# One group's input ahead of the heads, the other two beside the first projections

## The chip, the cores and the metric

One core of a Trainium2 chip runs the kernel. The core has five engines, each with its own queue of instructions: TensorE (PE: matrix multiplications and transposes, from SBUF into PSUM), VectorE (DVE), ScalarE (ACT), GpSimd (POOL) and SyncE (SP), which here only issues DMA transfers between HBM and SBUF. The metric is the device time of one execution in microseconds.

## What is computed

One streaming step of a small encoder of two layers, on 2048 rows of a prompt and 8 x 16 rows of samples, each row 1024 wide (17 tiles of 128 rows: 16 of the prompt, one of the samples). The part that matters here is the first layer, a gated DeltaNet with 8 heads:

```python
ada = c_act @ p["w_ada"][i] + p["b_ada"][i]
shift, scale, gate = jnp.split(ada[:, None, :], 3, axis=-1)
h = (rmsnorm(x, p["norm_pre"][i]) * (1.0 + scale) + shift)
# gdn_mixer
proj = h @ w_in                       # q, k, v (1024 columns each), z (1024), a and b (8 each)
qkv_c, new_buf = causal_conv(qkv, conv_buf, conv_w)
g = -jnp.exp(a_log) * jax.nn.softplus(a + dt_bias)
beta = jax.nn.sigmoid(b)
o, s_new = gdn_chunked(q, k, v, g, beta, s0, ...)   # per head: an inverse per block, then a scan over the blocks
o = rmsnorm(o, o_norm) * jax.nn.silu(z)
y = o @ w_out
```

The second layer is a differential attention; nothing of it is touched.

## The kernel before

The 17 tiles are handled in two halves. The first has nine, in three groups of three: group 0 is prompt tiles 0 and 1 and the sample tile, groups 1 and 2 are prompt tiles 2 to 4 and 5 to 7 (`HALVES`, lines 337 to 345). A half goes through `gdn_heads`, `out_proj`, `diff_heads` and `out_proj` again, each a stage of its own.

**The planner.** All stages are written as generators (streams), run by the class `Weave` (lines 88 to 327). It keeps a modelled time for each engine and each result, takes at every step the stream that can go on earliest (between equals the one with the higher priority, the last argument of `W.spawn`), and writes its instructions down. On PE, DVE, ACT and POOL the instructions run in the order in which they were written; on SP this holds only until `first_start` has ended (`W.ordered = False`, line 770). Places for tiles are rings: a stream that wants one waits until an earlier user has let go (`W.tile`, `W.keep`, `W.free`). `copy` and `either` (lines 206 to 219) choose the engine of a copy or of a subtraction by which is free in the model. `modulate` does so for ACT and DVE.

**The preparation, `first_start` (line 747).** It loads the weights of the adaptation for shift and scale of the first layer, 8 MB as eight transfers of 1 MB into a ring of four (`ada_load`), applies them (`ada_apply`, `ada_end`), and beside that runs `start` (line 729): for all three groups of the half, each tile's x (512 KB) is loaded into a ring of seven (`xn`), scaled by its norm (`scale_rows`: two squares on ACT, three small operations on POOL, one product on DVE), and, when a group's three tiles are there, turned into h: `h_parts` starts eight parts of 128 rows of hT. A part (`h_part`, line 673) transposes on PE into one of two PSUM banks (`TURN`), multiplies and adds (`modulate`, into one of two `htmp`), rounds to a first half (`W.copy`) and subtracts for a second half. The eighth part frees the x (lines 683 to 685). The result of a group is `hT` with the event `("w", "h", 0, half, gi)`. `first_start` also loads the first four of the heads' weight matrices (`gdn_loads(0)[:4]`, eight transfers of 256 KB through the two `st` buffers, each split by DVE, ACT and POOL). The stage ends when all this is written down; `vectors` (line 514) follows, a few small operations.

**The heads, `gdn_heads` (line 955).** `projections` (line 1023) goes over heads, in each over the three groups, in each over k, q, v: for each it waits for the group's hT and for the weights and does 24 matmuls (`mm3s`) into one of two banks (`PROJ`); `conv` then copies the result out into one of three `ub` buffers (`NU`), and convolves on DVE; for the sample tile it waits for the cached rows (`cached`, event `"cc"`). `gate_columns` (line 1060) does the columns of a and b for each of the three groups in turn, and after the third `gate_values` computes all gates (event `"gates"`), on which `keys`, `inverse` and `scans` of every head wait. q and k have five buffers each, freed by the scans. `others` (line 1007, the lowest priority) does the columns of z, 24 matmuls per tile and block, and the adaptation of later use; the weights for these come one after the other into the single place `wz` (`other_loads`, line 999).

Of the kernel before, what the change touches and what calls it, by code (L numbers as in the profile page):

```python
# [12 lines left out]
F32 = mybir.dt.float32  # L13
# [317 lines left out]
def body(ctx, tc, I, O):  # L331
# [341 lines left out]
    def h_part(l, half, gi, kt, xs, hT, temp, left):  # L673
        tiles = HALVES[half][gi]
        nt = len(tiles)
        n = nt * P
        for f in (1, 0):
            yield ("w", "A", l, f, kt // 4),
        ps = yield from bank_of(TURN)
        for i in range(nt):  # L680
            pe.transpose(ps[:, i * P:(i + 1) * P], cols_of(xs[tiles[i]], kt * P, P), ident)
        left["x"] -= 1
        if left["x"] == 0:
            for t in tiles:
                W.free(*(xs[t] if isinstance(xs[t], list) else [xs[t]]))
        ht = yield from temp()
        yield from modulate(l, kt, tiles, ht, ps)
        W.free(ps)
        yield from W.copy(hT[:, 0, kt, 0:n], ht[:, 0:n], n)
        e = W.either(n)  # L690
        yield e
        getattr(W, e).tensor_tensor(out=hT[:, 1, kt, 0:n], in0=ht[:, 0:n], in1=hT[:, 0, kt, 0:n].bitcast(F32),
                                    op=ALU.subtract)
        W.free(ht)
        left["h"] -= 1
        if left["h"] == 0:
            W.done(("w", "h", l, half, gi))
# [31 lines left out]
    def start(half, pool, nx):  # L729
# [10 lines left out]
        for gi, tiles in enumerate(HALVES[half]):  # L740
# [6 lines left out]
    def first_start(pool):  # L747
# [4 lines left out]
        def ada():  # L752
            for i, x in enumerate(todo):
                yield from ada_load(x, *x[2:], pool)
                if i == 0:
                    W.spawn(start(0, pool, 7), 3)
# [79 lines left out]
    def out_proj(l, hi_, groups, pool, ahead):  # L836
# [97 lines left out]
        if more:  # L934
            W.spawn(start(hi_ + 1, pool, 3), 1)
# [19 lines left out]
    def gdn_heads(hi_, tiles_of, pool, ahead):  # L955
# [15 lines left out]
        h_in = [hTs[0, hi_, gi] for gi in range(NGr)]  # L971
# [3 lines left out]
        def used_h(gi):  # L975
            uses[gi] -= 1
            if uses[gi] == 0:
                W.free(h_in[gi])
# [20 lines left out]
        def other_loads():  # L999
            for x in extras[:-1]:  # L1000
# [4 lines left out]
            yield from load_all(ahead[:1])  # L1005

        def others():
            for x in extras:
# [4 lines left out]
                for gi, tiles in enumerate(tiles_of):  # L1013
                    for i, t in enumerate(tiles):
                        ps = yield from bank()
                        yield from mm3s(ps[:, 0:WN], tok(h_in[gi], i), slots[x].cols(0, WN))
# [6 lines left out]
        def projections():  # L1023
            for h in range(H):
                for gi, tiles in enumerate(tiles_of):
# [3 lines left out]
                    for typ in (1, 0, 2):  # L1029
# [4 lines left out]
                                        lambda kt: (h_in[gi][:, 0, kt, 0:n], h_in[gi][:, 1, kt, 0:n]))  # L1034
# [25 lines left out]
        def gate_columns():  # L1060

            ab = pool.tile([P, MAXT, 2 * H], F32, name="ab", bufs=1)
            for gi, tiles in enumerate(tiles_of):
# [4 lines left out]
                for k4 in range(0, KT, 4):  # L1068
                    for i in range(2):
                        for q in range(4):  # L1070
                            pe.matmul(ps[32 * q:32 * q + 32, 0:n], wab[:, k4 + q, :],
                                      h_in[gi][:, i, k4 + q, 0:n].bitcast(F32),
# [556 lines left out]
        W.spawn(other_loads(), 5.5)  # L1629
        W.spawn(scans(), 5)  # L1630
# [562 lines left out]
```

## Time and profile before

| | us |
|---|---|
| median of three runs | 3585.93 |
| lowest, highest | 3585.64, 3587.45 |
| the profiled execution, its own time | 3588.79 |
| its span in the trace | 3587.0 |

Times in the trace are counted from the start of the span. Nearly every instruction is recorded through one helper (line 105), so the rows are told apart by tile names: `xn` is x, `htmp` a part of h before it is split, `hT` the result, `adaw` the adaptation's weights, `st` the staging of other weights, `wab` the weights of the gate columns, `wq` the weights of q, k and v, `wz` those of z. `ps<-hT,wq` is a projection, `ps<-cst_ident,xn` a transpose of x. PE is a matmul, PEld the load of its stationary operand, SPq the issue of a transfer.

### The profile page before, as it was taken

Reading aid. Unit: us, or ns where it says so; the run is one execution under the profiler, and the core shown is the slowest. Engines: PE = TensorE matmul, PEld = TensorE weight load, DVE = VectorE, ACT = ScalarE, POOL = GpSimd, SP = SyncE. Lnnn points to the kernel's source line nnn. Section 1 sums busy time; section 2 is a strip of 40 time slices with the busy share of each in tenths; the row PEclk is TensorE's granted clock in tenths of the full one; section 3 lists DMA queues with packets and bytes.
Section 4 is the critical chain, followed back from the end, with each engine's and each line's share of the span. In section 5 each row is a group of like instructions: output and inputs, shape, how many; then the busy total and the mean of one; then the engine's idle time right before and its main releaser. Section 6 shows DMA issues by size and latency. Waiting matters only on the chain.

```text
span 3587.0 us, 79525 instructions
## 1 busy us (share of the span) xinstructions
PE 3420.1 (95%) x29336; PEld 3178.8 (89%) x29336; DVE 2556.4 (71%) x6345; ACT 1773.7 (49%) x5379; POOL 1622.3 (45%) x2758
## 2 busy tenths in 40 slices
PE   5999999999999999999999999998899999999988
PEld 2887789889999999998989899888899999999988
DVE  4677788775576666666467877775588888888872
ACT  3454455553354444444445555553365555555541
POOL 4344444443444434443344654444455455554442
PEclk6999999999999999999999999999999999999999
DMA  5225422235343333344531222225311112111113
GB/s 190 59 72 158 122 76 73 58 99 189 127 125 108 112 112 115 111 119 120 180 93 47 59 58 75 61 72 162 124 42 55 29 56 57 50 52 34 51 59 124
DMA packets 479420, 330.61 MB, mean 92 GB/s; under 512 B 65799, under 2 KB 442143, under 8 KB 479030
## 3 DMA queue, kind: packets, MB, share of 16 engines
q1 hardware_dynamic: 474358, 316.76, 30.0%
q0 software_dynamic: 4672, 8.78, 1.0%
q8 instruction: 230, 3.77, 0.4%
q14 instruction: 160, 1.31, 0.1%
HBM read 233.65 MB, written 91.77 MB: 91 GB/s over the span
## 4 chain that ended last, share of the span: by engine, by line
PE 75%; DVE 11%; DMA 4%; POOL 4%; ACT 3%; issue 3%; SPq 0%; POOLq 0%; DVEq 0%; ACTq 0%
PE ps L105 75%; DVE negm L105 1%; DVE Lt L105 1%; DVE p L105 1%; POOL p L105 1%; POOL fo L105 1%; DVE wq L105 1%; POOL sm L105 1%; DVE Lr L105 1%; ACT L105 1%; ACT jkg L105 1%; SPq L105 0%; DVE Lw L105 0%; DVE at L105 0%; DVE r L105 0%
## 5 line engine op out<-in xcount | busy, mean ns | idle before, releaser
L105 PE MATMUL ps<-wq,hT 128*128 128x256 f32 x6120 | 853.3, 287 | 4.4 <-DVE r L105 3.4
L105 PEld LDWEIGHTS ps<-wq,hT 128*128 128x128 f32 x6120 | 775.3, 190 | 17.5 <-DVE r L105 4.5
L105 PE MATMUL ps<-hT,wq 128*128 128x384 f32 (+1 forms) x3456 | 697.5, 341 | 2.1 <-ACT ub L105 1.6
L105 PE MATMUL ps<-wz,hT 128*128 128x256 f32 x4488 | 648.8, 291 | 14.2 <-DVE r L105 13.4
L105 PEld LDWEIGHTS ps<-wz,hT 128*128 128x128 f32 x4488 | 581.3, 193 | 23.8 <-DVE r L105 14.8
L105 PEld LDWEIGHTS ps<-hT,wq 128*128 128x128 f32 x3456 | 558.1, 190 | 15.3 <-issue 2.9
L105 ACT ACTIVATE p<-ps,negm 128x512 f32<-128x512 f32 (+3 forms) x640 | 396.9, 624 | 240.5 <-DVE negm L105 235.5
L105 DVE TENSOR_REDUCE negm<-ps 128x1 f32<-128x512 f32 (+3 forms) x640 | 377.7, 606 | 48.3 <-PE ps L105 37.9
L105 POOL TENSOR_SCALAR p<-p,fj 128x512 f32<-128x512 f32 (+2 forms) x320 | 247.1, 782 | 231.8 <-DVE fj L105 179.2
L105 PE MATMUL ps<-kst,qst 128*128 128x512 f32 (+3 forms) x1280 | 347.1, 380 | 0.4 <-ACT p L105 0.4
L105 PE MATMUL ps<-vpc,at 128*128 128x128 f32 x2176 | 294.4, 277 | 4.6 <-DVE at L105 4.0
L105 DVE SCALAR_TENSOR_TENSOR p<-p,fj,p 128x512 f32<-128x512 f32 (+2 forms) x320 | 274.2, 882 | 27.9 <-POOL p L105 27.0
L105 PEld LDWEIGHTS ps<-vpc,at 128*128 128x128 f32 x2176 | 271.4, 192 | 15.2 <-DVE at L105 8.8
L105 PEld LDWEIGHTS ps<-kst,qst 128*128 128x128 f32 x1280 | 206.6, 190 | 18.2 <-ACT p L105 2.7
L105 PE MATMUL ps<-cst_ident,p 128*128 128x128 f32 x1224 | 194.0, 275 | 16.1 <-DVE p L105 12.1
L105 POOL TENSOR_TENSOR wq<-st,wq 128x512 fp32r<-128x512 f32 x103 | 142.6, 1386 | 144.6 <-ACT wq L105 72.4
L105 ACT COPY at<-ps 128x512 f32<-128x512 f32 (+1 forms) x208 | 106.4, 512 | 188.5 <-PE ps L105 187.2
L105 ACT ACTIVATE jk<-ps 128x128 f32<-128x128 f32 (+1 forms) x212 | 80.3, 379 | 229.6 <-PE ps L105 177.2
L105 POOL TENSOR_TENSOR fo<-fo,cpow 128x1 f32<-128x1 f32 x280 | 173.9, 621 | 23.3
L105 PEld LDWEIGHTS ps<-cst_ident,p 128*128 128x128 f32 x1224 | 144.0, 141 | 25.3 <-DVE p L105 15.1
L105 POOL TENSOR_TENSOR r<-r,r 128x256 f32<-128x256 f32 (+1 forms) x144 | 106.2, 758 | 108.5 <-DVE r L105 106.7
L105 POOL TENSOR_SCALAR fo<-so,sm 128x1 f32<-128x1 f32 x136 | 51.0, 375 | 211.2 <-ACT jkg L105 210.9
(334 smaller groups left out, 6519.2 us busy)
## 6 DMA issues: line engine op xcount, KB each, us to landing
st<-in_w_in_gdn_dram SPq DMA_DIRECT2D x128, 256.0 KB
st<-in_w_in_diff_dram SPq DMA_DIRECT2D x256, 128.0 KB
x<-x SPq DMA_DIRECT2D x34, 512.0 KB
wz<-in_w_ada_dram SPq DMA_DIRECT2D x16, 1024.0 KB
sp<-in_cache_k_dram SPq DMA_DIRECT2D x64, 256.0 KB
sp<-in_cache_v_dram SPq DMA_DIRECT2D x64, 256.0 KB
zg<-zt SPq DMA_DIRECT2D x68, 128.0 KB
og<-o SPq DMA_DIRECT2D x136, 64.0 KB
```

What stands on the lines that cost most here:

```text
L105: r = f(*args, **kw)
```

## The change

`first_start` prepares group 0 only, with three x buffers instead of seven. Groups 1 and 2 are prepared in `gdn_heads` by a new stream, `later_start` (priority 6.5), for the first half only. It takes one place that holds all three tiles of a group: for group 1 the place that hT of group 2 is written to later, for group 2 the place `wz`; it issues the three transfers and starts `later_rows` for each tile, which does the same `scale_rows` and `h_parts` as before, with a PSUM bank for the squares and `ub` buffers for the parts in place of `jk` and `htmp`. The eighth part frees the place as a whole (`"held"`). `other_loads` waits for the event that the transfers of group 2 have been issued, and then for `wz` to be free. hT is looked up when it is used, and not when the stage begins. The start of the second half's groups is as before.

```diff
--- before.py
+++ after.py
@@ -681,8 +681,11 @@
             pe.transpose(ps[:, i * P:(i + 1) * P], cols_of(xs[tiles[i]], kt * P, P), ident)
         left["x"] -= 1
         if left["x"] == 0:
-            for t in tiles:
-                W.free(*(xs[t] if isinstance(xs[t], list) else [xs[t]]))
+            if "held" in xs:
+                W.free(xs["held"])
+            else:
+                for t in tiles:
+                    W.free(*(xs[t] if isinstance(xs[t], list) else [xs[t]]))
         ht = yield from temp()
         yield from modulate(l, kt, tiles, ht, ps)
         W.free(ps)
@@ -726,7 +729,7 @@
         return (lambda: W.tile(pool, [P, 512], F32, "jk", 1, "s"),
                 lambda: W.tile(pool, [P, 384], F32, "htmp", 2, "v"))
 
-    def start(half, pool, nx):
+    def start(half, pool, nx, groups):
 
         xs = {}
         junk, temp = norm_places(pool)
@@ -737,7 +740,8 @@
             if not left:
                 yield from h_parts(0, half, gi, xs, temp)
 
-        for gi, tiles in enumerate(HALVES[half]):
+        for gi in groups:
+            tiles = HALVES[half][gi]
             left = set(tiles)
             for t in tiles:
                 x = xs[t] = yield from W.tile(pool, [P, D], F32, "xn", nx, "sy")
@@ -753,7 +757,7 @@
             for i, x in enumerate(todo):
                 yield from ada_load(x, *x[2:], pool)
                 if i == 0:
-                    W.spawn(start(0, pool, 7), 3)
+                    W.spawn(start(0, pool, 3, [0]), 3)
 
         def apply():
             for x in todo:
@@ -932,7 +936,7 @@
         W.spawn(collect(l, hi_, range(len(groups) - 1, len(groups)), 512, [lambda: new([P, 512], "ro", NR, "sy")] * 2,
                         lambda: bank_of(TURN)), 1)
         if more:
-            W.spawn(start(hi_ + 1, pool, 3), 1)
+            W.spawn(start(hi_ + 1, pool, 3, range(len(HALVES[hi_ + 1]))), 1)
         W.spawn(projections(), 0)
         W.run()
 
@@ -968,14 +972,13 @@
         if hi_ == 0:
             v.memset(tailsP, 0.0)
         U, gates = {}, {}
-        h_in = [hTs[0, hi_, gi] for gi in range(NGr)]
         uses = [2] * NGr
         rows_left = {t: H + 4 for ts in tiles_of for t in ts}
 
         def used_h(gi):
             uses[gi] -= 1
             if uses[gi] == 0:
-                W.free(h_in[gi])
+                W.free(hTs[0, hi_, gi])
 
         def row_done(t):
             rows_left[t] -= 1
@@ -997,12 +1000,34 @@
             yield from load(x, w_gdn, [(3072 + x[3] * WN, WN)], kind)
 
         def other_loads():
+            if hi_ == 0:
+                yield ("placed", NGr - 1), "sy"
             for x in extras[:-1]:
                 if x[1] == "ada":
                     yield from ada_load(x, *x[2:])
                 else:
                     yield from z_load(x, "wide")
             yield from load_all(ahead[:1])
+
+        def later_start():
+
+
+            places = (lambda: W.keep("hT2_0", lambda: tails[0].tile([P, 2 * KT * 384], F32, name="hT2", bufs=1), "sy"),
+                      lambda: W.tile(wpool, [P, 2 * KT * WN], F32, "wz", 1, "sy"))
+            for gi, place in zip((1, 2), places):
+                xs = dict(held=(yield from place()))
+                left = set(tiles_of[gi])
+                for i, t in enumerate(tiles_of[gi]):
+                    xs[t] = xs["held"][:, i * D:(i + 1) * D]
+                    sy.dma_start(xs[t], x_rows[t])
+                    W.spawn(later_rows(gi, t, xs, left), 3)
+                W.done(("placed", gi))
+
+        def later_rows(gi, t, xs, left):
+            yield from scale_rows(xs[t], bank)
+            left.remove(t)
+            if not left:
+                yield from h_parts(0, hi_, gi, xs, lambda: new([P, 388], "ub", NU, "v"))
 
         def others():
             for x in extras:
@@ -1013,7 +1038,7 @@
                 for gi, tiles in enumerate(tiles_of):
                     for i, t in enumerate(tiles):
                         ps = yield from bank()
-                        yield from mm3s(ps[:, 0:WN], tok(h_in[gi], i), slots[x].cols(0, WN))
+                        yield from mm3s(ps[:, 0:WN], tok(hTs[0, hi_, gi], i), slots[x].cols(0, WN))
                         W.spawn(gate_out(t, x[3], ps))
                         yield 0
                     if x == extras[-1]:
@@ -1031,7 +1056,7 @@
                         yield (key,)
                         ps = yield from bank_of(PROJ)
                         yield from mm3s(ps[:, 0:n], slots[key].cols(0, P),
-                                        lambda kt: (h_in[gi][:, 0, kt, 0:n], h_in[gi][:, 1, kt, 0:n]))
+                                        lambda kt: (hTs[0, hi_, gi][:, 0, kt, 0:n], hTs[0, hi_, gi][:, 1, kt, 0:n]))
                         if gi == NGr - 1:
                             W.free(slots[key])
                         W.spawn(conv(h, gi, typ, ps, d), 1)
@@ -1069,7 +1094,7 @@
                     for i in range(2):
                         for q in range(4):
                             pe.matmul(ps[32 * q:32 * q + 32, 0:n], wab[:, k4 + q, :],
-                                      h_in[gi][:, i, k4 + q, 0:n].bitcast(F32),
+                                      hTs[0, hi_, gi][:, i, k4 + q, 0:n].bitcast(F32),
                                       start=k4 == 0 and i == 0, stop=k4 > 0 and i == 1)
                 raw = yield from new([P, 384], "nv", NN, "s")
                 s.copy(raw[:, 0:n], ps[:, 0:n])
@@ -1627,6 +1652,8 @@
             W.spawn(cached(), 4)
         W.spawn(loads(), 6)
         W.spawn(other_loads(), 5.5)
+        if hi_ == 0:
+            W.spawn(later_start(), 6.5)
         W.spawn(scans(), 5)
         W.spawn(projections(), 0)
         W.spawn(others(), -1)
```

## Rows read from the trace of the kernel before

**Rows 1.** The page: TensorE over the span, and its granted clock in 40 slices.

```profile
PE 3420.1 (95%) x29336; PEld 3178.8 (89%) x29336; DVE 2556.4 (71%) x6345; ACT 1773.7 (49%) x5379; POOL 1622.3 (45%) x2758
...
PEclk6999999999999999999999999999999999999999
```

**Rows 2.** Stretches: length, busy us of each engine, granted clock, DMA share, GB/s.

```profile
30.00:35.00 5.00, 3.21 (x14) 1.33 (x15) 1.34 (x3) 1.37 (x3) 0.77 (x3) 0.50 1.04 396
...
55.00:69.00 14.00, 7.43 (x26) 4.02 (x24) 11.95 (x21) 6.43 (x13) 9.04 (x10) 0.50 0.26 69
...
60.00:80.00 20.00, 12.82 (x53) 6.94 (x57) 14.19 (x26) 8.86 (x17) 11.00 (x12) 0.50 0.23 64
...
69.00:81.00 12.00, 8.40 (x39) 4.21 (x43) 7.56 (x13) 5.44 (x9) 5.56 (x6) 0.50 0.22 63
...
155.00:265.00 110.00, 108.10 (x1088) 98.42 (x1086) 85.23 (x241) 59.40 (x193) 48.42 (x106) 1.00 0.22 55
```

**Rows 3.** Timeline of SP, 20 to 72 us: start, us, transfers issued, count.

```profile
20.40 5.01 SPq L105 DMA_DIRECT2D xn<-in_x_prompt_dram  x1
...
25.51 0.56 SPq L105 DMA_DIRECT2D adaw<-in_w_ada_dram  x1
...
26.12 3.02 SPq L105 DMA_DIRECT2D xn<-in_x_prompt_dram  x1
...
53.16 17.87 SPq L105 DMA_DIRECT2D st<-in_w_in_gdn_dram  x6
```

**Rows 4.** Timeline of all engines, 37 to 81 us (idle time before in brackets).

```profile
37.77 3.30 PE L105 MATMUL ps<-adaw,cT 128*32 128x512 f32 x16
...
44.39 0.56 ACT L105 ACTIVATE htmp<-ps,adaB,adaA 128x256 f32<-128x256 f32 x1 [1.28 <-DVE adaB L105]
...
56.08 1.50 DVE L105 TENSOR_TENSOR hT<-htmp,hT 128x384 fp32r<-128x384 f32 x1
...
68.22 1.11 POOL L105 TENSOR_TENSOR hT<-htmp,hT 128x384 fp32r<-128x384 f32 x1
...
79.84 0.56 DVE L105 TENSOR_TENSOR hT<-htmp,hT 128x384 fp32r<-128x384 f32 x1 [0.58 <-ACT hT L105]
```

**Rows 5.** Timeline of PE, 77 to 112 us: gate columns and first projections.

```profile
77.97 4.54 PE L105 MATMUL ps<-hT,wab 128*32 128x384 f32 x32
...
85.52 4.71 PE L105 MATMUL ps<-hT,wq 128*128 128x384 f32 x18
...
97.68 2.79 PE L105 MATMUL ps<-hT,wab 128*32 128x384 f32 x32
...
101.76 10.13 PE L105 MATMUL ps<-hT,wq 128*128 128x384 f32 x57
```

**Rows 6.** Timeline of DVE, 102 to 121 us: convolutions of group 0 and, last, group 1.

```profile
102.07 1.52 DVE L105 SCALAR_TENSOR_TENSOR k<-ub,taps,k 128x256 f32<-128x256 f32 x3
...
103.82 1.12 DVE L105 SCALAR_TENSOR_TENSOR k<-us,taps,k 128x128 f32<-128x128 f32 x3
...
105.62 0.56 DVE L105 SCALAR_TENSOR_TENSOR k<-ub,k 128x384 f32<-128x384 f32 x1
...
119.84 0.61 DVE L105 SCALAR_TENSOR_TENSOR k<-ub,taps,k 128x384 f32<-128x384 f32 x1
```

**Rows 7.** Instructions of x: durations in ns, least, median, most; first and last start.

```profile
L105 ACT ACTIVATE jk<-xn x34: 620/632/635, 16.7 to 1784.6; 128x512 f32<-128x512 f32 x34
...
L105 DVE TENSOR_SCALAR xn<-xn,rs x17: 746/755/1755, 19.4 to 1786.7; 128x1024 f32<-128x1024 f32 x17
```

**Rows 8.** Timeline, 118 and 175 us: last gate value, first step of a scan.

```profile
118.76 0.16 DVE L105 TENSOR_TENSOR g_eo<-g_neG,cst_ident 128x16 f32<-128x16 f32 x1
...
175.26 0.39 PE L105 MATMUL ps<-nv,Wf 128*128 128x128 f32 x2
```

**Rows 9.** Groups of PE from 155 to 265 us: count, busy us, mean ns.

```profile
L105 PE MATMUL ps<-hT,wq 128*128 128x384 f32 x216 | 45.8, 349 | 0.0
L105 PE MATMUL ps<-wz,hT 128*128 128x256 f32 x214 | 31.3, 291 | 0.0
```

## Prediction, made before the change had run

> **What bounds the kernel now.** Over the span TensorE (PE) is busy 95% of the time and its granted clock is full in every slice but the first [rows 1]. So the page says: TensorE-bound, except at the very start. I then read the stretches there one by one. From 60 to 80 us the engine is busy 12.82 us of 20 with 53 matmuls, and the granted clock is 0.50, the lower of its two levels (1.2 GHz) [rows 2]. What goes on then is in the list of events: the x of group 0 is turned into h until 57.6 us (the subtraction from 56.08), that of group 1 until 69.3, that of group 2 until 80.4 [rows 4]. Only then come the gate columns of group 0, put in at 77.97, and at 85.52 the first projections [rows 5]. Up to there nothing of the heads has been multiplied. The preparation itself is a chain between VectorE (DVE), ScalarE (ACT) and GpSimd (POOL): DVE is busy 11.95 us of 14 in group 1's stretch and 7.56 of 12 in group 2's, PE 7.43 and 8.40 [rows 2]. After 85.5 us PE hardly rests (108.10 of 110 us busy from 155 to 265) [rows 2]. So what can be won lies in front of 85.5 us: work of a TensorE-bound kernel, started while TensorE has next to nothing to do.
>
> **The change, part by part.** *Group 0 alone ahead.* All bytes are still moved, but the x that was issued at 20.40 and the one before it no longer go out ahead of the last adaptation weights at 25.51, and the one at 26.12 no longer shares the DMA engines with them [rows 3]. At the 396 GB/s of that stretch [rows 2], 1.0 to 1.5 MB is 2.5 to 3.8 us; I take 3. The last adaptation matmuls (37.77) and the second half of group 0's h (from 44.39) [rows 4] move by that, to 34.8 and 41.4. That second half is four parts of 128 rows of hT; it took 13.2 us (44.4 to 57.6), because the scaling of other groups' x and the splitting of weights stood in between. Group 1 took 11.7 us for eight parts, 1.5 us each, group 2 11.1. With 1.5 us, and some 0.7 us for the sample tile's two extra VectorE operations (an estimate from the 0.37 us of a 128-column operation [rows 6]), four parts are 8.8 us: group 0 is ready at about 50 instead of 57.6 (bounds 46 and 55).
>
> *Projections of head 0 beside the rest.* One head on one group is 3 x 24 = 72 matmuls. 57 took 10.13 us at full clock [rows 5], 0.178 us each, so 12.8 us for a group, and 25.6 us for groups 0 and 1 that can be done before group 2 is ready.
>
> *The six x moved.* On SP's queue they stand no longer in front of the first weight loads but behind the eight 256 KB loads of the first four weight matrices, each of which waits for one of two staging buffers. They go to the place that hT of group 2 will have, never used before, and to wz: no wait of their own. With the preparation over at about 50, their 3 MB land from 52 on at 396 GB/s, group 1's half by 54. If the queue lets them past a load that waits for its buffer, they land by 40; if the weight loads drag on as before (the last six from 53.16 to 71.0 [rows 3]), by 75. Per tile ACT then needs 2 x 0.63 us for the squares, POOL three small operations, DVE 0.75 us [rows 7]: some 5 us after the landing, at about 59, group 1's transposes start. POOL's and ACT's share of the scaling moves along; neither is the busier engine there. POOL's own DMA queue is not touched.
>
> *When group 2 is ready (T).* At the old pace groups 1 and 2 take 11.7 + 11.1 us: T = 82. But DVE now has the convolutions of groups 0 and 1 in the same stretch. One for group 0 is 1.52 for the prompt tiles, 4 x 0.37 for the sample tile and 0.56 at the end, 3.6 us; one for a full 384 columns is 3 x 0.61 + 0.56 = 2.4 [rows 6]; three of each are 18 us. The DVE gaps of the old stretches are 2.05 + 4.44 = 6.5 us [rows 2]. If nothing gives, T = 82 + 11.5 = 93; if ACT and POOL take over (the code picks the engine of a copy or a subtraction by which is free), 82. I take 90, since DVE was the busiest of the three in group 1's stretch; bounds 80, and 104 with the late x.
>
> *What T is worth to TensorE.* Before, everything from 85.5 on is left to do. After, at T, 25.6 us of projections are done and one more set of gate columns (2.79 [rows 5]). The gain is 85.5 + 25.6 + 2.8 - T = 114 - T: **24 us at T = 90**, 34 at 80, 10 at 104.
>
> *What T is worth to the chain of the heads.* No inverse and no scan starts before the gate values, and these need the columns of all three groups. The last gate columns started at 97.68 [rows 5], the last gate value at 118.76 [rows 8]: 21 us. From T = 90 that gives 111, **8 us earlier**; the 18 us of convolutions that are out of VectorE's way may add up to 5 before the first scan (175.3 before [rows 8]). This matters because from 155 to 265 only 216 projection matmuls run, three groups' worth in 110 us: the buffers of q, k and v are full until scans free them. TensorE lives then on the first z block, 214 of whose 216 matmuls fall there [rows 9]. If it arrives there 24 us sooner and the chain only 8 to 13, some 11 to 16 us more of filler are wanted. The next filler is the adaptation work, whose weights come through the single wz one at a time. So part of the 24 is lost there. I take the middle of 8 and 24: **a gain of 16 us**.
>
> *What costs nothing.* The wait that is added: other_loads waits until the x of group 2 is issued, then for wz. Behind it stand the z block's weights, all adaptation weights of later layers and, on PE, the z and adaptation matmuls, which have the lowest priority. With wz free at about 88 and four loads of some 4 us (an estimate: six took 17.87 us [rows 3], 3 us each, and 1 us for company) the z weights are there at 105, and the z matmuls fell almost all behind 155 [rows 9]. It is uncovered only if T passes about 130. The wait that is moved: projections wait for h of their group; behind it on PE stand later heads, which need the same groups.
>
> **Against a rule on the clock.** From 55 to 81 us TensorE was more than half busy, with transposes, and stayed at 0.50 [rows 2]; the 18 projections that began at 85.52 took 4.71 us instead of 18 x 0.178 = 3.2 [rows 5]. A start from the low level cost 1.5 us here. With the change the projections of groups 0 and 1 may each begin so: 3 us instead of 1.5, well within my bounds. The Trainium skill (TensorE: Matmul & The Clock Gate, Part 4: PE-mode transpose) says that transposes do not count as busy for the clock; the rows at 0.50 agree. By that rule the pause between the groups, filled with transposes only, puts the clock down again, which the clock rival below prices.
>
> **The rivals.**
> - *The chain decides all* (the gain is what the gates gain): 0 to 8 us, 3578 to 3586. For it speaks that projections are paced by scans from 155 on; against it that TensorE is busy 108 of 110 us there, so that work done earlier is work missing later.
> - *The clock stays low in the whole interleaved stretch.* At 2 x 0.178 us group 0's 72 matmuls take 25.6 us, which the wait for group 1 hides (50 to 76); group 1's take 12.8 more, not hidden: 24 - 13 = 11 by TensorE, 8 by the chain, about 10 us, 3576. Against it: 57 in 10.13 us some 16 us after the first projection.
> - *Slower: the last group comes too late.* The h parts of groups 1 and 2 now share three temporaries with the convolutions, and group 0's convolutions hold theirs until the cached rows are in. Before, two temporaries gave a part every 1.45 us; with one left, a part comes every 2.9: 16 parts are 46 us, T = 59 + 46 = 105, the gates at 126, 7 us later than before, 3593. With the late x on top, T = 126, 12 us lost by TensorE and 28 by the chain, 3598 to 3614. It decides from T = 98 on, where the gates come no earlier than before. For it: DVE was the busiest engine of the old stretch. Against it: the convolutions of group 0 let go of theirs once the cached rows are in.
> - *It does not do what it says*: x lands so late, or the fixed order of PE lets projections wait behind transposes of x, that nothing overlaps: T = 98 or so and no projections ahead of it, no change, 3580 to 3590.
>
> **How the numbers follow.** The profiled execution took 3588.79 us (span 3587.0), 2.9 above the median of the runs, 3585.93. The sum on it: 3588.8 - 16 = 3572.8; on the median 3570. Chances: the forecast (10 to 27 us won, 3559 to 3576) 0.50; T near 80 and all of it kept (27 to 34 won) 0.08; chain or low clock (0 to 10 won) 0.22; no overlap 0.08; slower 0.12. The range reaches from 3554, T near 82 with nearly all kept, to 3589; left out are the slower rival and the best end. A difference under 0.2%, 7.2 us, is about what a measurement of this kernel cannot tell from none. Faster by more (below 3578.8): the first two and a third of the chain or clock cases, 0.65. Slower by more (above 3593.1): the slower rival and a little for orders that shift later on, 0.13. The same: 0.22.
>
> **What the profile after would show.** Right: first projections at 50 to 55 us with hT of group 0, some 140 done when group 2's last subtraction ends at 80 to 100; the last gate value at 100 to 115; the end 10 to 27 us earlier, nearly all of it already there at 300 us. Wrong: PE idle over 10 us between 110 and 270 (the chain); granted clock 0.50 through group 1's projections (the clock); h parts that wait for a temporary, and T past 98 (the slower rival); x of group 1 landing after 65.

## The result, and the profile after

The changed kernel takes 3641.74 us (median; 3635.39 to 3648.55) beside 3586.69 us for the kernel before on the same chip: ratio 1.0152, 95% interval 1.0131 to 1.0172. It is slower by 55 us, where 16 us were to be won.

The page of the changed kernel, which answers to [rows 1]: TensorE's work over the span and its granted clock.

```profile
PE 3441.9 (95%) x29336; PEld 3197.8 (88%) x29336; DVE 2560.2 (70%) x6338; ACT 1767.9 (49%) x5376; POOL 1630.7 (45%) x2764
...
PEclk7998999999999999999999999999999999999999
```

The page says no more than before: 95% busy, TensorE-bound. Only the fourth slice of the clock (273 to 364 us) is lower. So the question is which stretch lost. Stretches of the kernel before (from, to, length, busy us and instructions of PE, PEld, DVE, ACT and POOL, granted clock, DMA share, GB/s):

```profile
0.00:220.00 220.00, 177.47 (x1335) 142.42 (x1336) 132.50 (x351) 96.39 (x261) 86.09 (x171) 0.86 0.36 108
220.00:960.00 740.00, 716.08 (x6419) 647.45 (x6418) 545.84 (x1457) 363.79 (x1163) 327.29 (x681) 0.98 0.38 109
960.00:2000.00 1040.00, 1013.62 (x9053) 964.35 (x9053) 688.03 (x1771) 492.40 (x1493) 448.26 (x762) 1.00 0.39 113
...
220.00:260.00 40.00, 40.00 (x361) 37.70 (x360) 35.09 (x95) 26.09 (x87) 26.56 (x58) 1.00 0.32 81
260.00:300.00 40.00, 37.72 (x342) 29.38 (x341) 27.24 (x81) 17.35 (x58) 11.71 (x33) 0.96 0.62 200
300.00:400.00 100.00, 93.88 (x797) 77.41 (x797) 75.34 (x217) 45.31 (x160) 45.19 (x102) 0.91 0.48 142
```

The same stretches of the changed kernel:

```profile
0.00:220.00 220.00, 178.96 (x1351) 148.77 (x1351) 133.76 (x339) 93.16 (x251) 80.56 (x166) 0.88 0.36 107
220.00:960.00 740.00, 681.75 (x5966) 605.91 (x5965) 519.58 (x1419) 345.21 (x1132) 318.55 (x661) 0.95 0.35 102
960.00:2000.00 1040.00, 1015.95 (x9006) 969.39 (x9006) 672.94 (x1694) 477.89 (x1423) 445.61 (x728) 0.99 0.39 116
...
220.00:260.00 40.00, 28.23 (x225) 19.93 (x224) 17.58 (x43) 13.17 (x48) 10.48 (x21) 0.79 0.60 198
260.00:300.00 40.00, 35.89 (x230) 31.71 (x229) 29.87 (x88) 20.57 (x74) 21.48 (x61) 0.91 0.41 123
300.00:400.00 100.00, 87.86 (x764) 70.25 (x764) 65.60 (x190) 39.04 (x135) 34.33 (x77) 0.90 0.41 129
```

Up to 220 us the changed kernel is slightly ahead: 16 more matmuls, at a clock of 0.88 instead of 0.86. From 960 on the two are alike. Between 220 and 960 TensorE does 453 matmuls fewer in the same 740 us: it is idle for 58.3 us instead of 23.9, which is 34 us, and its mean clock is 0.95 instead of 0.98. Between the levels 0.5 and 1, that is some 74 us at the lower level instead of 30, so another 22 us of full-speed work (an estimate from clocks of two digits). Together 56 us: the whole loss, and none of it lies where the change was made. The pages bear it out over the whole span: the same 29336 matmuls keep TensorE busy 21.8 us longer, and of the 52.5 us between the two spans (3639.5 and 3587.0) the other 30.7 are idle time. By 820 us nearly all of it is there: the last of the first half's 1728 projections starts at 819.3 instead of 767.6. The deepest part is 220 to 260, in which 28.23 us of 40 are busy at 0.79, before 40.00 at 1.00.

The early part went like this (timeline of all engines in order of time; start, us, engine, instruction, in brackets the idle time before it and what ended it):

```profile
51.11 8.60 PE L105 MATMUL ps<-hT,wq 128*128 128x384 f32 x48
...
55.62 0.62 ACT L105 CAST wq<-st 128x512 fp32r<-128x512 f32 x1 [6.40 <-DMA st<-in_w_in_gdn_dram]
...
60.50 0.62 ACT L105 CAST wq<-st 128x512 fp32r<-128x512 f32 x1 [4.26 <-DMA st<-in_w_in_gdn_dram]
61.13 1.28 ACT L105 ACT_TABLE_LOAD   x1
...
64.55 0.61 ACT L105 ACTIVATE ps<-hT 128x512 f32<-128x512 f32 x1
...
89.62 1.54 PE L105 MATMUL ps<-cst_ident,wz 128*128 128x128 f32 x6 [2.79 <-DVE ub L105]
...
102.52 1.25 DVE L105 TENSOR_TENSOR hT<-ub,hT 128x384 fp32r<-128x384 f32 x1
...
106.68 2.79 PE L105 MATMUL ps<-hT,wab 128*32 128x384 f32 x32
...
128.48 0.17 DVE L105 TENSOR_TENSOR g_eo<-g_neG,cst_ident 128x16 f32<-128x16 f32 x1
...
184.12 0.39 PE L105 MATMUL ps<-nv,Wf 128*128 128x128 f32 x2
```

The first projections start at 51.11, group 0 being ready. The first square of group 1's x (`ps<-hT`: x lies in the place of hT) runs only at 64.55, though SP had issued that x at 36.40 and 42.23, and it starts with no wait of its own: ACT was at the splits of the weights until 61.1, two of which waited 6.40 and 4.26 us for their transfers, and then at a table load and the vectors. Group 2 is ready at 103.8 (before 80.4, [rows 4]), the last gate columns start at 106.68 (97.68, [rows 5]), the last gate value comes at 128.48 and the first scan step at 184.12 (118.76 and 175.26, [rows 8]). So the chain of the heads is 9 to 10 us late.

### The profile page after: what moved, and what is told of

Its sections match the earlier page's. It is cut to its first block, busy times and chain, and to the rows that moved or that the text cites. A ratio compares the mean times of both kernels' runs of the same rounds, so it can differ in the third digit from the quotient of the medians.

```text
span 3639.5 us, 79489 instructions
## 1 busy us (share of the span) xinstructions
PE 3441.9 (95%) x29336; PEld 3197.8 (88%) x29336; DVE 2560.2 (70%) x6338; ACT 1767.9 (49%) x5376; POOL 1630.7 (45%) x2764
## 4 chain that ended last, share of the span: by engine, by line
PE 72%; DVE 11%; DMA 7%; POOL 4%; issue 3%; ACT 2%; SPq 1%; POOLq 0%; DVEq 0%; ACTq 0%
PE ps L105 72%; DVE negm L105 1%; DVE Lt L105 1%; DVE p L105 1%; POOL p L105 1%; POOL fo L105 1%; DMA st<-in_w_in_gdn_dram 1%; SPq L105 1%; POOL sm L105 1%; DVE Lw L105 1%; DVE wq L105 1%; DVE Lr L105 0%; DVE r L105 0%; DMA wz<-in_w_ada_dram 0%; DVE hT L105 0%
## 5 line engine op out<-in xcount | busy, mean ns | idle before, releaser
L105 ACT ACTIVATE jk<-ps 128x128 f32<-128x128 f32 (+1 forms) x212 | 80.3, 379 | 229.6 <-PE ps L105 176.8
```

The source lines that it names most:

```text
L105: r = f(*args, **kw)
```

## The experiments

Three theories in turn. *L*: the late chain makes the loss. *O*: the rest of the stage runs in another order (the planner writes it anew for each kernel), and that of before happened to be good. *S*: SP and both staging buffers are held, and the next weights come late. After these fell or fell short: *F*, the place of the adaptation's matmuls in TensorE's order, against *H*, a hole that any filler only covers. In each diff the lines are those of the kernel named; `...` stands for lines left out.

**The kernel before in another order.** Only a price in the planner is changed, for the first half's heads.

```diff
         U, gates = {}, {}
+        if hi_ == 0:
+            W.HOP = {k: dict(x) for k, x in Weave.HOP.items()}
+            W.HOP['v']['pe'] += 8
...
+        W.HOP = Weave.HOP
```

> The kernel before, with one number of the planner changed for the first half's heads alone: the modelled delay from VectorE to TensorE is 264 instead of 256 ns. The work is the same, only the order in which the planner writes it down changes somewhat. Theory L (late chain: the changed kernel loses its time because the hidden states of groups 1 and 2, and with them the gates, come later, 128.5 us against 118.8) expects the time of before: 3580 to 3595. Theory O (order: the kernel before has an order that happens to be good, and any new order of this stage gives it up) expects 10 to 40 us more, 3597 to 3627.

3603.59 us, ratio 1.0040 (1.0024 to 1.0055), with the last gate value at 118.37 and the first scan step at 175.27, as before. A change of nothing but order costs 14 us. The second such order:

```diff
+            W.HOP['pe']['v'] += 8
...
+        W.HOP = Weave.HOP
```

> The kernel before with the edit of changed_reordered_2. With before and before_reordered it gives three orders of the kernel before, to set against three of the changed kernel. O: 3580 to 3610, early stage (last gate value at 118.5, first scan step at 175) as before. L says nothing of an order's price beyond the 14 us seen: within 14 us of 3588.

3604.82 us, 1.0045 (1.0027 to 1.0063). So the order of before is the best of the three, and up to some 15 us of the 55 may be no more than that it was given up. (Not every new order costs this: some versions below come to 3582 to 3595 us.)

**The changed kernel in the same two orders.**

> The changed kernel, with the same tiny edit as before_reordered (the planner's price for a hop from VectorE to TensorE is 264 ns instead of 256 for the first half's heads; nothing else). It asks how much of the 55 us belongs to the particular order that the planner chose. Theory L (the late chain: squares of group 1 at 64.5, gates at 128.5) expects the early stage unchanged and the end where the changed kernel's was, 3630 to 3655. Theory O (an unlucky order of the rest) expects the same early stage and an end well earlier, 3590 to 3620.

> The changed kernel with another such edit: the hop from TensorE to VectorE is priced at 204 instead of 196 for the first half's heads. L: 3630 to 3655 again. O: three orders of the changed kernel (with changed_reordered) spread over 20 us or more, and the middle of them lies 10 to 30 us above the orders of the kernel before (3588, 3604 and before_reordered_2), which would be what the change costs by itself.

3654.25 us (1.0176, 1.0161 to 1.0191) and 3639.06 us (1.0127, 1.0105 to 1.0149). They stay where the changed kernel was, 35 to 50 us above the two other orders of before; the spread of 15 us is as large as among those. O explains a part only. The hole from 220 us on is in both, for instance in the second:

```profile
220.00:260.00 40.00, 29.12 (x241) 21.21 (x239) 20.14 (x47) 13.55 (x49) 10.55 (x21) 0.83 0.61 198
```

**No weights ahead** (changed kernel): the first four weight matrices are not loaded and split in `first_start`.

```diff
-            yield from load_all(gdn_loads(0)[:4])
+            yield from load_all(gdn_loads(0)[:0])
```

> The changed kernel, with none of the heads' first four weight matrices loaded ahead of the heads (they are loaded there, in the same order, after the x of groups 1 and 2 have been issued). In the changed kernel their splitting keeps ACT's queue until 61.8 us, in front of the squares of group 1, whose x is there some 12 us sooner. Theory L expects the squares at about 50, the last gate value 10 or more us earlier than 128.5, and a time of 3590 to 3610, most of the loss gone. Theory O expects 3625 to 3655, as the order is a new one in any case.

3583.47 us, 0.9979 (0.9962 to 0.9995): all of the loss is gone, and a little is won. From its timeline (ACT, PE, DVE):

```profile
50.40 0.58 ACT L105 ACTIVATE ps<-hT 128x512 f32<-128x512 f32 x1
...
59.15 0.49 PE L105 MATMUL ps<-cst_ident,hT 128*128 128x128 f32 x3
...
83.70 0.55 PE L105 MATMUL ps<-cst_ident,wz 128*128 128x128 f32 x3
...
90.43 2.79 PE L105 MATMUL ps<-hT,wab 128*32 128x384 f32 x32
...
113.57 0.17 DVE L105 TENSOR_TENSOR g_eo<-g_neG,cst_ident 128x16 f32<-128x16 f32 x1
...
180.76 0.63 PE L105 MATMUL ps<-nv,Wf 128*128 128x128 f32 x2
```

The squares run 14 us earlier, the sixteen parts of groups 1 and 2 take 24.5 us (59.15 to 83.70) although projections and convolutions run beside them, and the last gate columns start at 90.43. In two more orders it was 3589.02 us (0.9992, 0.9982 to 1.0002) and 3582.25 us (0.9979, 0.9964 to 0.9993), the second with ScalarE's hop to TensorE 8 ns up:

> no_weights_ahead (no weights of the heads loaded and split ahead of them) with the edit of before_reordered. It asks whether its 3583 us was a lucky order or comes from the earlier squares of group 1 (50.4 instead of 64.5). L: early stage as in no_weights_ahead (last gate columns at about 90), 3575 to 3595. O: it scatters like the others, 3570 to 3610, and a value above 3600 would say that the recovery of 58 us was partly luck.

> no_weights_ahead in another order (the planner's price for a hop from ScalarE to TensorE 8 ns up). It asks for the third order of that version, and whether one beats both kernels clearly. All theories: early stage as in no_weights_ahead; 3570 to 3592.

So this is no lucky order: three of three stand at the kernel before or up to 7.5 us below it (the interval of the middle one takes in 1), and no other version does. It says that loading and splitting weights ahead of x costs the time; it doesn't say by which way.

**Two groups ahead** (changed kernel): group 1 is prepared in `first_start` again, only group 2 later.

```diff
-                    W.spawn(start(0, pool, 3, [0]), 3)
+                    W.spawn(start(0, pool, 6, [0, 1]), 3)
...
-            for gi, place in zip((1, 2), places):
+            for gi, place in list(zip((1, 2), places))[1:]:
```

> Half of the change: groups 0 and 1 are prepared ahead of the heads, as before, and only group 2 beside the first projections, its x in wz. Theory L expects hT of group 2 ready at about 90 instead of 104 (80 before), gates at 112 to 118 and 3580 to 3600. Theory O expects 3600 to 3650. If it is the z weights that suffer, since their place holds x of group 2 here as well, it is as slow as the whole change, 3640.

3595.20 us, 1.0013 (1.0001 to 1.0025). The time is in the range that L gave, but not by L's way: the gates come at 121.6, later than L said and 3 us later than before, and the first scan step at 188.56, 13 us later than before and 4 later than in the changed kernel, and still it is 46 us faster than that. This speaks against L.

**Own temporaries** (changed kernel): the h parts of groups 1 and 2 use the unused end of the place that holds their x, not `ub`; the place is freed after the last part instead of after the last transpose (those lines are left out).

```diff
+                xs["tmp"] = [xs["held"][:, 3 * D + i * 384:3 * D + (i + 1) * 384] for i in range(2)]
...
-                yield from h_parts(0, hi_, gi, xs, lambda: new([P, 388], "ub", NU, "v"))
+                yield from h_parts(0, hi_, gi, xs, lambda: W.hold(xs["tmp"], ("tmp", gi), "v"))
```

> The changed kernel, but the h parts of groups 1 and 2 have two temporaries of their own again, in the unused end of the place that holds their x (which is freed after the last part instead of after the last transpose), and no longer share the three ub buffers with the convolutions. Parts came every 2.0 us in the changed kernel against 1.4 before. Theory L expects a part every 1.5 us, group 2 ready at about 95, gates at 117 to 120, and 3600 to 3620. Theory O expects no less than 3625. If the weights in front of group 1 are what makes it late, and not the temporaries, under 8 us are won.

3604.84 us, 1.0045 (1.0030 to 1.0061), 37 us faster than the changed kernel, in the range that L gave, but again not by L's way: the last gate columns start at 106.25 and the last gate value comes at 128.71, as late as in the changed kernel. The shared buffers are not what makes group 2 late. And a kernel with that late chain can be 37 us faster: once more against L, and against O's 3625 or more as well.

**Late gates alone** (kernel before): the gate columns of group 2 wait for a projection, nothing else.

```diff
                         W.spawn(conv(h, gi, typ, ps, d), 1)
+                        if hi_ == 0 and (h, gi, typ) == (0, 1, 1):
+                            W.done(("late",))
...
                 yield ("w", "h", 0, hi_, gi),
+                if hi_ == 0 and gi == NGr - 1:
+                    yield ("late",),
```

> The kernel before, with the gate columns of group 2 made to wait for the second projection of head 0 on group 1 (at about 119 us): the gates come some 10 us late, as in the changed kernel, and nothing else is moved. L: the last gate value at 128 to 130, first scan step at 183 to 186, and 25 to 55 us slower (3613 to 3643), as the changed kernel. S: the fillers cover most of it, 0 to 15 us slower than the other orders of before (3588 to 3618).

3594.91 us, 1.0017 (1.0002 to 1.0032), with the last gate value at 129.43 and the first scan step at 183.31, which is the chain of the changed kernel. Ten us of delay cost 6 us (1 to 11) against the order of before, and nothing against its other two. L has fallen.

**The z weights later.** In the changed kernel SP issues nothing between 74.37 and 106.89. Its waits from 60 to 200 us (what it waited for: us in all, times, longest):

```profile
SPq L105 <- POOL wz L105: 37.3, 3, 32.1
```

The first two loads of the z block sit in both staging buffers, and can't be split into `wz` before the x of group 2 has left it. So the z loads were made to wait for h of group 2 (changed kernel):

```diff
             if hi_ == 0:
-                yield ("placed", NGr - 1), "sy"
+                yield ("w", "h", 0, hi_, NGr - 1), "sy"
```

> The changed kernel with one wait put elsewhere: the z weights are no longer loaded as soon as the x of group 2 has been issued, but once h of group 2 is ready. So their two loads don't sit in the staging buffers while wz is still full of x, and SP isn't held from 74.4 to 106.9; the early stage (squares at 64.5, gates at 128) is left late. Theory L (the late chain makes the loss): 3630 to 3650, nothing won. Theory S (the weights of the next heads come late because SP and both staging buffers are held for 32 us): 3600 to 3625, projections of the second head's last group at about 235 to 245 instead of 262.

3595.42 us, 1.0019 (1.0003 to 1.0035): 46 us won, more than S expected, and yet the hold that S blames is not the cause, for SP was still held:

```profile
75.37 0.39 SPq L105 DMA_DIRECT2D S<-in_state_gdn_dram  x1
109.20 0.36 SPq L105 DMA_DIRECT2D st<-in_consts_dram  x1
```

The transfers are put on SP's queue in an order that the generators don't fix after `first_start`, and it didn't change; the last gate value came at 129.63. Only what was written down behind that moved, and the hole is gone. The last projection of the second head now starts at 236.0 instead of 261.5, as S had said, and the next transfer of a head's weights goes out at 216.68 instead of 232.89. So the other half of S, weights of the next heads that come late, is not refuted by this run.

```profile
220.00:260.00 40.00, 38.45 (x322) 32.77 (x321) 29.38 (x85) 23.08 (x85) 23.39 (x53) 1.00 0.47 139
```

The same wait in the kernel before:

```diff
         def other_loads():
+            if hi_ == 0:
+                yield ("w", "h", 0, hi_, NGr - 1), "sy"
```

> The kernel before with the z weights waiting for h of group 2, as they do in effect in the changed kernel, but without anything held: it asks what a later z block costs by itself. Both theories: last gate value at 118 to 119, and between 3585 and 3610, the scatter of the orders of before; more than that would put the late z block itself among the causes.

3601.93 us, 1.0037 (1.0018 to 1.0055), as the other orders of before: no cost of the waiting z block shows beyond that of a new order.

**The place of the adaptation.** What stands in the hole of the changed kernel (timeline of PE from 219 us):

```profile
219.02 1.23 PE L105 MATMUL ps<-wz,hT 128*128 128x256 f32 x9
225.59 1.94 PE L105 MATMUL ps<-wz,cT 128*32 128x512 f32 x8 [5.34 <-DMA wz<-in_w_ada_dram]
227.45 0.80 PE L105 MATMUL ps<-y,Wf 128*128 128x128 f32 x2
...
248.99 1.02 PE L105 MATMUL ps<-cst_ident,adaC 128*9 128x128 f32 x4 [5.04 <-DVE adaC L105]
249.80 0.64 PE L105 MATMUL ps<-y,Wf 128*128 128x128 f32 x2
...
289.41 2.29 PE L105 MATMUL ps<-hT,wq 128*128 128x384 f32 x6 [4.11 <-ACT us L105]
```

The first z block ends at 220 and leaves `wz`; the first adaptation weights are issued at 220.28, and their matmuls stand next in TensorE's fixed order. They wait 5.34 us, and a step of the scan (`y,Wf`) waits behind them: its y was ready at 219.83, 7.6 us before it could run. The filler that ought to fill the waits of the scan has the scan wait for it. The Trainium skill (PSUM — Partial Sum Buffer, Engine vs sequencer instructions) states that matmuls start and complete in program order. These rows agree: the scan's two begin at 227.45, right behind the eight at 225.59. The other two waits have other causes (timelines of DVE and ACT):

```profile
219.50 0.33 DVE L105 SCALAR_TENSOR_TENSOR y<-ps,g_neG,nv 128x128 f32<-128x128 f32 x1
...
247.44 0.43 DVE L105 CAST wq<-st 128x512 fp32r<-128x512 f32 x1 [6.42 <-DMA st<-in_w_in_gdn_dram]
...
248.85 0.34 DVE L105 SCALAR_TENSOR_TENSOR y<-ps,g_neG,nv 128x128 f32<-128x128 f32 x1
...
287.92 0.28 ACT L105 ACTIVATE o<-ps 128x128 f32<-128x128 f32 x1 [4.27 <-DMA og<-o]
```

At 248.99 TensorE waits for an adaptation result (`adaC`), but DVE was held by a cast of a head's weight until 247.44, and the scan's own next y, at 248.85, stood behind that cast too. The cast waited for a transfer issued at 241.02, between two of 1 MB for the adaptation at 240.53 and 241.56. So this wait is one for a head's weight, which is late as S had it. The wait at 289.41 is a projection's, for a copy on ACT that stood behind a wait for the transfer of an earlier result. In the kernel before, the z block ends at 264, and the longest wait for adaptation weights up to 300 us is 2.21 us. To test the place of the adaptation, its weights were made to wait for the second weight of the third head (changed kernel):

```diff
             for x in extras[:-1]:
+                if x == ("w", "ada", 0, 2, 0):
+                    yield ("w", "gdn", 0, 0, 2), "sy"
```

> The changed kernel, in which the first of the adaptation weights wait until the second weight of the third head is split (before: they went out as soon as the first z block had left wz, at 220.3). Nothing ahead of 200 us is touched. Theory F (TensorE is held from 220 to 260 by the adaptation's matmuls, which stand in its fixed order ahead of the scan's and wait 5.3 us for their weights and 5.0 us for adaC, and by the low clock that follows): 3595 to 3625, TensorE busy over 34 us of 40 from 220 to 260 (28.2 in the changed kernel). Rival H (the heads' chain itself is late and leaves a hole, whatever fills it): 3630 to 3655, and the hole stays.

3606.85 us, 1.0046 (1.0026 to 1.0065), 35 us won with gates at 130.36. No stall of 5 us is left; the longest at 220 to 260 is 2.42 us, for a scan's own V:

```profile
220.00:260.00 40.00, 34.98 (x277) 31.59 (x276) 27.82 (x76) 23.36 (x89) 19.37 (x42) 0.91 0.49 137
```

F's forecast holds, H's in part: 5 us of the hole stay. But the edit does two things at once: it moves the adaptation's matmuls, and it lets the heads' weights out first (their next transfers at 224.36, 228.38 and 233.14 instead of 232.89, 241.02 and 248.62). How much each gives was not separated. With the wait for the third weight of that head, `("w", "gdn", 0, 2, 2)`:

> The same with the adaptation weights waiting for the third, last weight of the third head. It moves the adaptation further back. F: no stall of 5 us at its matmuls between 220 and 260 either, 3595 to 3625; a time above 3630 without such stalls there would go against F, and for H. H: 3630 to 3660.

3624.95 us, 1.0102 (1.0065 to 1.0138), at the upper end of what F allowed. The hole at 220 is as shallow as in the run before it, but there is another later on, at adaptation weights again (4.5 us in two waits) and at the lower clock:

```profile
220.00:260.00 40.00, 35.83 (x277) 31.33 (x277) 29.44 (x85) 21.40 (x82) 24.40 (x53) 0.87 0.44 132
...
400.00:450.00 50.00, 43.28 (x321) 33.80 (x314) 29.21 (x75) 18.55 (x64) 17.52 (x31) 0.69 0.35 102
```

All of them side by side (us; the head column is the start of the second head's last projection, the hole is TensorE's busy time from 220 to 260 and its clock; the kernel before gave medians of 3585 to 3592 beside the different runs, so differences of a few us between rows say nothing):

| kernel | time | last gate value | first scan step | second head's last projection | busy of 40, clock |
|---|---|---|---|---|---|
| before | 3586.7 | 118.8 | 175.3 | 233.0 | 40.0, 1.00 |
| before_reordered | 3603.6 | 118.4 | 175.3 | 229.6 | 38.5, 1.00 |
| before_reordered_2 | 3604.8 | 118.1 | 174.4 | 232.2 | 40.0, 1.00 |
| before_late_z | 3601.9 | 117.7 | 169.1 | 220.0 | 38.8, 1.00 |
| before_late_gates | 3594.9 | 129.4 | 183.3 | 239.4 | 38.5, 1.00 |
| changed | 3641.7 | 128.5 | 184.1 | 261.5 | 28.2, 0.79 |
| changed_reordered | 3654.3 | 130.9 | 183.4 | 259.7 | 29.3, 0.83 |
| changed_reordered_2 | 3639.1 | 130.8 | 185.8 | 260.9 | 29.1, 0.83 |
| changed_ada_waits_2 | 3625.0 | 129.3 | 181.5 | 239.7 | 35.8, 0.87 |
| changed_ada_waits | 3606.9 | 130.4 | 184.3 | 243.3 | 35.0, 0.91 |
| own_temporaries | 3604.8 | 128.7 | 184.5 | 232.2 | 39.6, 1.00 |
| changed_z_waits | 3595.4 | 129.6 | 183.5 | 236.0 | 38.5, 1.00 |
| two_groups_ahead | 3595.2 | 121.6 | 188.6 | 245.7 | 37.5, 0.96 |
| no_weights_ahead | 3583.5 | 113.6 | 180.8 | 230.3 | 37.3, 0.96 |
| no_weights_reordered | 3589.0 | 115.1 | 181.8 | 232.6 | 37.6, 0.96 |
| no_weights_reordered_2 | 3582.3 | 115.7 | 181.9 | 233.3 | 37.6, 0.96 |

With gates at 128 to 131 the kernels lie anywhere between 3595 and 3654 us, so the gates don't set the time. The four with a clock below 0.9 from 220 to 260 are the four above 3620. Between 200 and 300 us the three orders of the changed kernel, and no others, have both long waits (5.3 to 5.6 us for the adaptation's weights, 5.8 to 6.4 us of DVE for a head's weight), and in them alone the second head ends at 260 to 262.

## Why the prediction was wrong

*Where the time is to be won* was right: TensorE's idle stretch ahead of 85.5 us, and group 0 ready at 50 (50.3 in the trace), with projections from 51.11.

*"With the preparation over at about 50" was wrong.* The x did not come late: SP let it past the weight loads that waited for their buffers, and its six transfers were issued from 36.4 to 49.3. But the weights' splits stand ahead of the squares in ACT's fixed order, and ACT was held by them until 61.1: squares at 64.55, not at about 54. I had counted each queue that x is moved past on SP, not those that its arithmetic is moved past on ACT and DVE. no_weights_ahead shows the size: 50.4, and the gates 15 us earlier.

*T, 90, bounds 80 to 104, was 103.8*: at the upper bound, by the squares that came 14 us late against the 50.4 without the splits. It was not the three shared `ub` buffers, as the slower rival had it; own_temporaries has its last gate columns at 106.25. In no_weights_ahead they start at 90.43, so with the preparation over at 50, T is about 89 and the gates come at 113.6: my 90 and 111. What that is worth can be read there as far as that version stands for it (its first weights come later, too): 7.5 us (0.9979; 2 to 14 by the interval), and 3 and 7.5 in its other orders, not 16. That is the size that the rival *the chain decides all* gives; the first scan step came at 180.8 there in spite of the early gates, and why was not settled.

*"What T is worth to TensorE" had a term too large.* The sum takes all 144 projections of groups 0 and 1, 25.6 us, as done by T. At 103.8 the changed kernel had started 101 of them, and no_weights_ahead 105 at its T of 89.2: 18 to 19 us at 0.178 each. So the sum with the measured term gives some 2.5 us instead of 10 at T = 104, and 18 instead of 25 at T = 89. Up to 220 us the changed kernel had done 16 more matmuls at a clock higher by 0.02, by an estimate some 6 us of work. So much was won, and then lost.

*"So part of the 24 is lost there" was the step that failed most.* I saw that projections are paced by scans after 155 and that the next filler's weights come one at a time through `wz`, and took the worst that this could do as a gain that shrinks. But an early filler that isn't there doesn't only leave TensorE idle. Its matmuls are written into TensorE's order at a fixed place, and the scan steps behind them wait too: 5.34 us at 225.59. And its weights go out ahead of the heads' own, one of which then held DVE, and with it the scan, for 6.42 us (5.04 of them idle on TensorE). These two are 10.4 of the 15.9 us idle between 220 and 300; another 4.11 have to do with neither. The lower clock beside them costs at most 12 (0.79 and 0.91 over 40 us each are 24 us at the lower level, some of them idle in any case). The kernel before loses some 4 us there, so the difference is 20 to 24 us; up to 960 us it is 56, and the rest isn't in one place.

*"What costs nothing": the added wait, uncovered only if T passes about 130.* The z matmuls indeed were not late (the first at 140.6 instead of 154.5). That the z loads would take both staging buffers, so that SP stands still for 32 us, I had not seen; changed_z_waits, where SP stands still as long, shows that this alone does not cost the time.

*The slower rival* had T past 98 and gates 7 us late, and priced it at 7 us, 3593; with the late x, 3598 to 3614. T and gates came about where it said (103.8, 9.7 us late), but by luck: the late squares made them late, not the temporaries. And before_late_gates, which has just those late gates and nothing else, gives 3594.9. Its price for what it described was right. What it lacked, like the forecast, was any term for the order of the rest: up to 16 us between orders of before alone, and the hole of the changed kernel.

*The clock.* The 48 projections from 51.11 took 8.60 us, 0.179 us each, the price of the full clock [rows 5]. The clock then fell, as that rival had it: TensorE stood for 5 us and did little but small transposes up to 75, and the remaining 24 projections of group 0 took some 6.6 us instead of 4.3. Stretches of the changed kernel, columns as above:

```profile
51.00:60.00 9.00, 8.71 (x49) 8.28 (x48) 2.88 (x4) 0.62 (x1) 3.87 (x3) 1.00 0.55 173
60.00:75.00 15.00, 7.55 (x41) 6.02 (x42) 8.50 (x23) 12.01 (x33) 7.61 (x20) 0.58 0.25 72
75.00:82.00 7.00, 6.91 (x32) 6.37 (x31) 6.54 (x13) 1.95 (x4) 3.57 (x9) 0.68 0.28 76
```

The fall cost 2 to 3 us there, where that rival had 13. The Trainium skill's rule on transposes (TensorE: Matmul & The Clock Gate, Part 4: PE-mode transpose), which stood behind that rival, agrees with the 0.58, though TensorE was also idle for half of that stretch, which this row can't tell apart from transposes. In no_weights_ahead, with projections between the transposes, 59 to 84 us are at 1.00:

```profile
59.00:84.00 25.00, 23.37 (x173) 19.39 (x172) 24.06 (x44) 13.97 (x30) 14.34 (x21) 1.00 0.35 94
```

What is settled: the late squares came from the weights' splits on ACT; without those the loss is gone in three orders of three; the late chain alone costs 6 us; the order of before is better by 14 to 16 us than two that differ in nothing else; the place of the adaptation in the order goes with most of the hole from 220 on, and moving it gives back 35 and 17 us, by the medians, the second hardly more than orders alone make. What stays open: how that divides between its matmuls, which the scan has to wait for, and its transfers, behind which the heads' weights come late; and how the 46 us of changed_z_waits divide between this hole and a better order behind 300 us. No run held the rest of the order fixed.

## What to carry to other kernels

Work that is moved behind a stage is moved behind that stage's arithmetic too: list what stands ahead of it on each engine, not only on the queue that brings its data; here the splits of four weights, early for no need, cost 14 us at the start. Where a planner writes fixed orders, low-priority work with late data is not free: in order, it stops what stands behind it, on the engine and on the queue of transfers; look at the first instruction after each filler has run out, and at the transfer that it needs. And before a difference of a few tenths of a per cent is put down to a change, run the kernel before in an order that differs in nothing: here that alone was worth 14 to 16 us.

## What had not been expected

A price changed by 8 ns in the planner moved the kernel before by 16 us (0.4%) with gates and first scan step within 1 us of where they were, while the changed kernel kept its loss in three orders (3639 to 3654 us). Ten us of delay in the gates, on which every scan waits, cost 6 us. And a loss of 55 us in a kernel that is 95% busy left that 95% as it was: only the table by stretches and the clock beside it showed where it went.
